# Output gates of a gated-linear-attention layer as one seven-product scheme on token tiles

## The chip, the cores and the metric

The kernel runs on one NeuronCore of a Trainium2 chip. The metric is the device time of one execution in microseconds (us). A core has a matrix engine (TensorE, "PE" in the profile; its weight loads are "PEld"), a vector engine (VectorE, "DVE"), a scalar engine (ScalarE, "ACT"), a general engine (GpSimd, "POOL") and an engine that here only issues transfers (SyncE, "SP"). Each has its own instruction queue, worked off in order. The engines share an on-chip memory; matmul results land in banks of 128 x 512 float32 numbers, from which DVE or ACT fetch them. Transfers (DMA) are issued from an engine's queue and run beside the engines.

## The reference

The computation is one layer of a decoder with 512 tokens and width 1024, in float32: a layer norm, then gated linear attention (GLA, 4 heads) and latent attention (MLA, 8 heads) side by side on the same normalised rows `h`, merged by two sigmoid gates, an output product, a layer norm, a squared-ReLU network of width 4096 and a last layer norm. What matters here is the GLA branch:

```python
q_g, k_g, v_g, r_g, a_lr, q_lat, kv_lat, gate_logits = jnp.split(h @ w_in, offsets, axis=-1)
log_a = log_sigmoid(a_lr @ w_gla_a2 + b_gla_a2) / 16
o_gla = gla_chunked(q_g * HK ** -0.5, k_g, v_g, log_a)      # per head
o_gla = rms_norm(o_gla, gla_norm_g)
y_gla = (o_gla * jax.nn.silu(r_g)) @ w_o_gla
```

`r_g`, the output gates, is the product of `h` (512 x 1024) and 1024 columns of `w_in` (1024 x 1024), and goes through silu. `v_g` has the same shape.

## The kernel before

**Products and pieces.** A float32 product is made of three matmuls on parts: each operand is split into a rounded high part and a low part, and high x high, high x low and low x high are summed in a bank. The parts of `h` are in `hT` (feature rows in partitions, tokens in columns). Weights come as a stream of pieces of 512 KB, planned in the order in which they are used (`plan`, `stream`). For each piece SP issues the load (`fetch`, two ahead of the piece in use), ACT writes the high part (`whi`, L189) and DVE the low part (`wlo`, L190). `pump(i)`, called where PE reaches piece i, emits the load and the split of the pieces that come next; the split of a piece is emitted one ahead, and `whi` and `wlo` have two buffers each.

**Stages.** In order: layer norm of the input; `lat` (the latent columns); `q`; `k`; then `v` and `r` in turn, half of the 1024 columns at a time: `proj_v(0)`, `proj_r(0)`, `proj_v(1)`, `proj_r(1)`; then the merge gates (`g`, and the units `g0` and `g1`), `y_gla`, MLA, the output product and the network.

**Token-tile products.** `proj_v` and `proj_r` use `gemm_tm` (L279 to L281): for each of 8 k-tiles of 128 features and each of 4 token tiles, three matmuls of 128x512, whose streaming operand is the weight. So one half of r is 4 pieces and 96 matmuls, 24 to a piece. The bank of a token tile is then read by `e`: ACT makes a tanh, and DVE two `scalar_tensor_tensor` that write the gates of two heads into `Rg[h]`.

**Work between the matmuls.** GLA's own work is written as generators: `gla_levels(h)` builds, per head, the decay masks in levels s = 2, 4, ..., 256 and the scores (POOL steps L680 and L681, ACT exponentials L686, DVE products M L688, small matmuls L742 and L746, masked copies L698 on DVE), and `gla_out(h)` multiplies scores with v and forms the gated rows. `spawn` puts a generator in a list, and `tick` lets the first few of them emit their next step; the products call `tick` every third token tile (`fine=3`). So the order of all engines' instructions is fixed when the program is built, by where the ticks fall; `finish` runs a generator to its end at that place.

**The seven-product scheme that is there already.** The units `g0`, `g1` compute a gate product from sums of operand blocks: the k rows and columns are taken as 2 x 2 blocks, and seven block products, with weights such as "12" plus "11" (t1), replace eight. The sums of weights are made by transfers: a load of one block, then an accumulating transfer from POOL's queue onto the same tile (`u_load`). The sums of `h` are made in `h_early`: per pair of k-tiles DVE adds and subtracts, splits each sum in two parts, and writes them to an off-chip scratch `hsd`, from which `h_load` reads them later. Results of products are combined in banks, and by ACT copies (L1072) and DVE additions or subtractions (L1068). Within g0 `tick(3)` is called after each second k.

Of the kernel before, what the change touches and what calls it, by code (L numbers as in the profile page):

```python
# [10 lines left out]
F32 = mybir.dt.float32  # L11
# [5 lines left out]
ALU = mybir.AluOpType  # L17
# [35 lines left out]
def tile_hybrid_block(ctx: ExitStack, tc: tile.TileContext, I, out, dbg=None):  # L53
# [23 lines left out]
    def B(shape, dt=F32, n="b"):  # L77
        return pb.tile(shape, dt, tag="B", name=nm(n))
# [4 lines left out]
    def DR(shape, n):  # L83
        n = nm(n)
        return pd.tile(shape, F32, tag=n, name=n)
# [7 lines left out]
    def f(ap):  # L93
        return ap.bitcast(F32)
# [207 lines left out]
        PL["lat", i] = plan("w_in", C_A + i * half, half, res=True)  # L302
    PL["q"] = plan("w_in", C_Q, T)
    PL["k"] = plan("w_in", C_K, T)
    for hp in range(2):
        PL["v", hp] = plan("w_in", C_V + hp * T, T)
        PL["r", hp] = plan("w_in", C_R + hp * T, T)
    def plan_qr(g):
        PL["qr", g] = plan("w_q_b", NOPE, 4 * ROPE, heads=(HQ, 4 * g, 4))

    PL["g", 0] = plan("w_in", C_G, T)

    WQ = {}
    HOME = {"w": ("whi", "wlo"), "r": ("wraw", "wraw"), "a": ("xh", "xl")}
    FMO = (("11", 0), ("21", 1), ("t1", 2), ("22", 5), ("t2", 3), ("t3", 6), ("t4", 4))
    HELD = (("21", "f1"), ("21", "g0"), ("22", "g0"))
# [329 lines left out]
                split(ps[:, i * HV:(i + 1) * HV], Vh[h][0][:, a, :], Vh[h][1][:, a, :])  # L646
        gemm_tm([PL["v", hp]], hT, T, e, guard=guard, fine=3)

    def proj_r(hp):
        hs = (2 * hp, 2 * hp + 1)  # L650

        def e(a, j, ps):
            th = B([P, T], F32, "th")
            act(th, ps, AF.Tanh, scale=0.5)
            for i, h in enumerate(hs):
                if Rg[h] is None:
                    Rg[h] = A([P, NT, HV], F32, "rg")
                stt(Rg[h][:, a, :], th[:, i * HV:(i + 1) * HV], 1.0, ps[:, i * HV:(i + 1) * HV],
                    op0=ALU.add, op1=ALU.mult)
        gemm_tm([PL["r", hp]], hT, T, e, fine=3)  # L660

    SS = [None] * GH

# [99 lines left out]
        yield  # L763

    def gla_out(h):
        while SS[h] is None or Vh[h] is None or Rg[h] is None:
            yield
        sd, s128, s256 = SS[h]

# [172 lines left out]
    hsd = []  # L942

    def h_early():
        for p in range(4):
            raw = [B([P, T], F32, "hraw") for _ in range(2)]
            for i in range(2):
                h = hT[2 * p + i]
                vtt(raw[i], f(h[:, 0]), f(h[:, 1]), op=ALU.add)
            yield  # L950
            a11, a12, a21, a22 = raw[0][:, :256], raw[1][:, :256], raw[0][:, 256:], raw[1][:, 256:]
            X = [B([P, 2, 256], F32, "hx") for _ in range(2)]
            vtt(X[0][:, 0], a21, a22, op=ALU.subtract)
            vtt(X[0][:, 1], X[0][:, 0], a11, op=ALU.subtract)
            vtt(X[1][:, 0], a12, X[0][:, 1], op=ALU.add)
            vtt(X[1][:, 1], a11, a21, op=ALU.subtract)
            yield
            for x in X:
                xs = [B([P, 2, 256], F32R, "sh") for _ in range(2)]
                split(x, *xs)  # L960
                hsd.append([DR([P, 2, 256], "hsd") for _ in range(2)])
                for t, d in zip(xs, hsd[-1]):
                    nc.sync.dma_start(d, f(t))
                yield

    t_ln1 = spawn(ln_in1())
# [1 line left out]
    for hf in range(2):  # L968
        if hf == 1:
            finish(t_ln1)  # L970
            t_prep = spawn(prep())
        for i in range(2):
            gemm_tm([PL["lat", i]], hT, half, ev_lat(i), tts=(2 * hf, 2 * hf + 1))
    t_lat = spawn(latents())
    gemm_fm(PL["q"], hT, T, ev_q)
    t_lat2 = spawn(latents2())
    t_he = spawn(h_early())
    gemm_fm(PL["k"], hT, T, ev_k)
    finish(t_prep, t_lat)
    lv = [False] * GH  # L980
# [15 lines left out]

    WID[0] = 3
    proj_v(0)
    proj_r(0)
    finish(t_lat2)  # L1000
    proj_v(1, lambda: levels_upto(1))
    proj_r(1)
    t_gla = [t_lv, t_out]


# [32 lines left out]
    def unit(key, ops, evac, after=None, pb=None):  # L1038
# [3 lines left out]
        def prod(op):  # L1042
            ph = dict(FMO)[op]
            opens = ph in (0, 2, 1)
            for g in range(UNITS[key][2]):
# [6 lines left out]
                for k in range(4):  # L1052
                    while len(ops) <= k:
                        tick(3)
                    xh, xl = ops[k][ph]
                    for a in range(2):
                        c = slice(a * P, (a + 1) * P)
                        oa = o[:, a * 256:(a + 1) * 256]
                        mm(oa, hi[:, k, c], xh, start=opens and k == 0 and a == 0, stop=False, skip_group_check=True)  # L1059
                        mm(oa, hi[:, k, c], xl, start=False, stop=False, skip_group_check=True)  # L1060
                        mm(oa, lo[:, k, c], xh, start=False, stop=k == 3, skip_group_check=True)  # L1061
                    if k % 2:
                        tick(3)
                if ph == 0:
                    e1[g] = B([P, T], F32, "e1")
# [45 lines left out]
    def h_load():  # L1111
        for p in range(4):
            o = {0: (0, 0), 1: (1, 0), 4: (1, 1)}
            o = {ph: tuple(part(hT[2 * p + i], w, slice(256 * h, 256 * h + 256)) for w in range(2))
                 for ph, (i, h) in o.items()}
            for i in range(2):
                xh, xl = [B([P, 2, 256], F32R, "sh") for _ in range(2)]
                for t, d in zip((xh, xl), hsd[2 * p + i]):
                    nc.sync.dma_start(f(t), d)
                o[(2, 5)[i]], o[(3, 6)[i]] = (xh[:, 0], xl[:, 0]), (xh[:, 1], xl[:, 1])  # L1120
            hops.append(o)
            yield

    finish(t_he)
    spawn(h_load())
    u_load("g0", "t1")
    u_load("g0", "22")
# [17 lines left out]
    prods = {"g0": unit("g0", hops, ev_gate0, after0), "g1": unit("g1", hops, ev_gate, after)}  # L1145
    for key, op in GATES:
        prods[key](op)
        if op == "t3" and key == "g0":
            finish(*t_gla)
    hT = hops = None  # L1150

# [380 lines left out]
```

## Time and profile before

| what | value |
|---|---|
| median of three runs | 893.7 us (893.48 to 894.96) |
| the profiled execution | 894.09 us, span 892.3 us |
| granted PE clock in it | 0.997 |
| PE busy | 875.2 us, 98% of the span |
| DVE busy | 619.0 us, 69% |
| ACT busy | 459.4 us, 51% |
| POOL busy | 168.0 us, 19% |
| bytes moved | 119.38 MB |

The span is the time from the first to the last instruction of the profiled execution; it lies within the time of the run. An instruction is named by its line, its engine, its operation, and by what it writes and reads (`wlo<-wraw,whi`); "px" and "mm" are result banks. A row of groups gives the busy time, the mean duration of one in ns, and the idle time of the engine before them with what ended it. Matmuls overlap in PE's pipeline, so the time that one costs is the distance between two starts, not its length. The line numbers are those of the kernel before; in the changed kernel those of the shared helpers are the same or 19 higher, and those behind the new functions some 95 higher.

### The profile page before, as it was taken

Reading aid. Unit: us, or ns where it says so; the run is one execution under the profiler, and the core shown is the slowest. Engines: PE = TensorE matmul, PEld = TensorE weight load, DVE = VectorE, ACT = ScalarE, POOL = GpSimd, SP = SyncE. Lnnn points to the kernel's source line nnn. Section 1 sums busy time; section 2 is a strip of 40 time slices with the busy share of each in tenths; the row PEclk is TensorE's granted clock in tenths of the full one; section 3 lists DMA queues with packets and bytes.
Section 4 is the critical chain, followed back from the end, with each engine's and each line's share of the span. In section 5 each row is a group of like instructions: output and inputs, shape, how many; then the busy total and the mean of one; then the engine's idle time right before and its main releaser. Section 6 shows DMA issues by size and latency. Waiting matters only on the chain.

```text
span 892.3 us, 12880 instructions
## 1 busy us (share of the span) xinstructions
PE 875.2 (98%) x4868; PEld 762.5 (85%) x4868; DVE 619.0 (69%) x1002; ACT 459.4 (51%) x808; POOL 168.0 (19%) x192
## 2 busy tenths in 40 slices
PE   6999999999999999999999999999999999999996
PEld 5988888888899988888888888988888888889985
DVE  7838987568365745657756797887556646787865
ACT  6456554455365543445644424365457546656720
POOL 1003555436120010100000002003500520131000
PEclk9999999999999999999999999999999999999998
DMA  7416632212997423121207618005950990399312
GB/s 247 121 47 200 225 119 72 71 48 68 305 272 195 124 89 112 38 60 54 96 24 273 197 48 306 2 1 122 308 136 9 273 257 29 79 230 235 118 65 79
DMA packets 80254, 119.38 MB, mean 134 GB/s; under 512 B 8464, under 2 KB 46224, under 8 KB 80192
## 3 DMA queue, kind: packets, MB, share of 16 engines
q1 hardware_dynamic: 63680, 85.54, 30.0%
q0 software_dynamic: 14592, 29.37, 14.7%
q10 hardware_dynamic: 1920, 3.66, 1.1%
q8 instruction: 38, 0.62, 0.3%
q14 instruction: 24, 0.20, 0.1%
HBM read 97.04 MB, written 8.91 MB: 119 GB/s over the span
## 4 chain that ended last, share of the span: by engine, by line
PE 94%; DVE 3%; DMA 1%; issue 1%; ACT 0%; POOLq 0%; DVEq 0%
PE mm L245 12%; PE mm L247 12%; PE mm L246 12%; PE mm L279 7%; PE mm L280 7%; PE mm L281 7%; PE mm L1061 3%; PE mm L1060 3%; PE mm L1059 3%; PE px L1344 2%; PE px L1345 2%; PE px L1343 2%; PE mm L1344 2%; PE mm L1345 2%; PE mm L1343 2%; PE px L742 2%
## 5 line engine op out<-in xcount | busy, mean ns | idle before, releaser
L190 DVE TENSOR_TENSOR wlo<-wraw,whi 128x1024 fp32r<-128x1024 f32 (+2 forms) x95 | 105.4, 1109 | 108.4 <-ACT whi L189 103.9
L189 ACT ACTIVATE whi<-wraw 128x1024 fp32r<-128x1024 f32 (+2 forms) x95 | 90.7, 955 | 89.5 <-PE mm L246 36.6
L245 PE MATMUL mm<-h,whi 128*128 128x512 f32 x256 | 99.9, 391 | 0.0
L246 PE MATMUL mm<-h,whi 128*128 128x512 f32 x256 | 99.9, 390 | 0.0
L247 PE MATMUL mm<-h,wlo 128*128 128x512 f32 x256 | 95.5, 389 | 0.0
L1362 POOL DMA_DIRECT2D res<-ev x42 | 37.3, 1008 | 179.0 <-ACT ev L1360 154.7
L190 DVE TENSOR_TENSOR wlo<-wq,whi 128x1024 fp32r<-128x1024 f32 x36 | 44.1, 1225 | 27.0 <-ACT whi L189 26.8
L247 PEld LDWEIGHTS mm<-h,wlo 128*128 128x128 f32 x256 | 48.1, 188 | 10.0
L245 PEld LDWEIGHTS mm<-h,whi 128*128 128x128 f32 x256 | 48.1, 188 | 9.7
L246 PEld LDWEIGHTS mm<-h,whi 128*128 128x128 f32 x256 | 48.1, 188 | 9.6
L189 ACT ACTIVATE whi<-wq 128x1024 fp32r<-128x1024 f32 x36 | 38.1, 1058 | 26.2 <-PE mm L1060 14.3
L279 PE MATMUL mm<-whi,h 128*128 128x512 f32 x128 | 50.7, 409 | 0.0
L280 PE MATMUL mm<-wlo,h 128*128 128x512 f32 x128 | 50.5, 395 | 0.0
L281 PE MATMUL mm<-whi,h 128*128 128x512 f32 x128 | 50.2, 394 | 0.0
L1060 PE MATMUL mm<-sh,whi 128*128 128x256 f32 x160 | 45.3, 283 | 0.0
L1059 PE MATMUL mm<-sh,whi 128*128 128x256 f32 x160 | 45.3, 283 | 0.0
L1061 PE MATMUL mm<-sh,wlo 128*128 128x256 f32 x160 | 45.3, 283 | 0.0
L189 ACT ACTIVATE xh<-wraw 128x1024 fp32r<-128x1024 f32 (+1 forms) x28 | 27.4, 987 | 29.2 <-PE mm L281 15.9
L190 DVE TENSOR_TENSOR xl<-wraw,xh 128x1024 fp32r<-128x1024 f32 (+1 forms) x28 | 31.3, 1130 | 9.6 <-ACT xh L189 9.5
L686 ACT ACTIVATE E<-rp 128x256 f32<-128x256 f32 x64 | 26.1, 417 | 22.7 <-POOL rp L681 13.9
L1405 ACT ACTIVATE relu<-mm 128x512 f32<-128x512 f32 x24 | 14.1, 596 | 41.8 <-PE mm L247 41.8
L409 POOL TENSOR_TENSOR mv<-mv,mhalf 128x1 f32<-128x1 f32 x4 | 3.3, 837 | 170.3 <-DVE mv L408 170.3
(433 smaller groups left out, 2662.8 us busy)
## 6 DMA issues: line engine op xcount, KB each, us to landing
wraw<-in_w_ff_dram SPq DMA_DIRECT2D x36, 512.0 KB, 5.2
wraw<-in_w_in_dram SPq DMA_DIRECT2D x35, 512.0 KB, 3.5
wq<-in_w_ff_dram POOLq DMA_DIRECT2D x26, 512.0 KB, 9.5
res<-ev POOLq DMA_DIRECT2D x42, 256.0 KB, 9.8
wq<-in_w_in_dram SPq DMA_DIRECT2D x10, 512.0 KB, 5.5
hsd<-sh SPq DMA_DIRECT2D x16, 256.0 KB, 2.6
sh<-hsd SPq DMA_DIRECT2D x16, 256.0 KB, 5.3
wraw<-in_w_o_gla_dram SPq DMA_DIRECT2D x8, 512.0 KB, 3.7
```

The source lines that it names most:

```text
L189: st["ins"] = act(hi[:, :nk, :n], raw[:, :nk, :n], AF.Copy)
L190: st["lo"] = vtt(lo[:, :nk, :n], raw[:, :nk, :n], f(hi[:, :nk, :n]), op=ALU.subtract)
L245: mm(o, hi[:, c], xh, start=first, stop=False)
L246: mm(o, hi[:, c], xl, start=False, stop=False)
L247: mm(o, lo[:, c], xh, start=False, stop=last)
L279: mm(o, xh, hi[:, :n], start=opens, stop=False, skip_group_check=share)
L280: mm(o, xh, lo[:, :n], start=False, stop=False, skip_group_check=share)
L281: mm(o, xl, hi[:, :n], start=False, stop=last, skip_group_check=share)
L1059: mm(oa, hi[:, k, c], xh, start=opens and k == 0 and a == 0, stop=False, skip_group_check=True)
L1060: mm(oa, hi[:, k, c], xl, start=False, stop=False, skip_group_check=True)
L1061: mm(oa, lo[:, k, c], xh, start=False, stop=k == 3, skip_group_check=True)
L1362: nc.gpsimd.dma_start(res[tt + t][:, j * T:(j + 1) * T], e, accum_op=ALU.add)
```

## The change

The two calls of `proj_r` become one. The 512 x 1024 x 1024 product of r is taken as 2 x 2 blocks in tokens (two halves of 256), k (even and odd k-tiles) and columns (two halves of 512), and done as seven block products in place of eight (`RW`: the weight operands 11, 21, t2, t1, t3, 22, t4, each with a phase that names its operand of `h`). A block product is two pieces, of 12 matmuls of 128x512 each (two k-tiles, two token tiles, three matmuls). So 14 pieces and 168 matmuls stand for 8 pieces and 192 matmuls.

- The weight sums t1 to t4 are made by transfers. `r_load` (SP) brings block 12 into the tiles of t2, t1 and t3, `r_acc` (POOL) accumulates blocks 11 and 22 on them: six loads and eight accumulating transfers, emitted by the generator `r_prep` in the second half of the latent product and after. t4 is t2 plus block 21: two more accumulating transfers onto t2's tiles, emitted after product t1 (`RA4`).
- `h_early` is emitted before q and not after it (it idles for six ticks first), splits per 256 columns (16 splits, 16 writes), and must be done before r. r reads the sums back into tiles "xr" (16 reads of 256 KB, one product ahead); `h_load` reads them again for g0 and g1, as before.
- Results are combined in two banks per token half, with six ACT copies ("er") and six DVE additions or subtractions on 128x512, and then go through the same tanh and products (`silu`).
- The order is v0, all of r, v1. `gla_out(h)` waits, at build time, until all four token tiles of its gates have been emitted (`rgn`). In r `tick` is called three times per product (`RT`).
- In g0 `tick(3)` is called only after the last k, and GLA's generators are finished after product t4 and not after t3.

The matmul count of the whole program falls by 24, all of 128x512; ACT gets 20 instructions more, DVE 20, SP 20 transfers, POOL 10.

```diff
@@ -302,15 +302,34 @@
         PL["lat", i] = plan("w_in", C_A + i * half, half, res=True)
     PL["q"] = plan("w_in", C_Q, T)
     PL["k"] = plan("w_in", C_K, T)
-    for hp in range(2):
-        PL["v", hp] = plan("w_in", C_V + hp * T, T)
-        PL["r", hp] = plan("w_in", C_R + hp * T, T)
+    WQ = {}
+
+    RY, RT, RA4 = (4, 4, 2, 2, 1, 2, 2), ((0, 0), (1, 0), (1, 1)), "t1"
+    RW = (("11", 0), ("21", 1), ("t2", 3), ("t1", 2), ("t3", 6), ("22", 5), ("t4", 4))
+
+    def r_src(op, hf):
+        i, j = int(op[0]) - 1, int(op[1]) - 1
+        c0 = C_R + j * T
+        return I["w_in"].rearrange("(k p) n -> p k n", p=P)[:, 4 * hf + i:4 * hf + i + 3:2, c0:c0 + T]
+
+    PL["v", 0] = plan("w_in", C_V, T)
+    PL["r"] = []
+    for op, _ in RW:
+        for hf in range(2):
+            PL["r"].append(len(stream))
+            e = {"nk": 2, "n": T, "res": False}
+            if op[0] == "t":
+                e["src"] = lambda q=("r", op, hf): WQ[q]
+            else:
+                e["dmas"] = [(slice(0, 2), r_src(op, hf), None)]
+            stream.append(e)
+    PL["v", 1] = plan("w_in", C_V + T, T)
+
     def plan_qr(g):
         PL["qr", g] = plan("w_q_b", NOPE, 4 * ROPE, heads=(HQ, 4 * g, 4))
 
     PL["g", 0] = plan("w_in", C_G, T)
 
-    WQ = {}
     HOME = {"w": ("whi", "wlo"), "r": ("wraw", "wraw"), "a": ("xh", "xl")}
     FMO = (("11", 0), ("21", 1), ("t1", 2), ("22", 5), ("t2", 3), ("t3", 6), ("t4", 4))
     HELD = (("21", "f1"), ("21", "g0"), ("22", "g0"))
@@ -646,18 +665,94 @@
                 split(ps[:, i * HV:(i + 1) * HV], Vh[h][0][:, a, :], Vh[h][1][:, a, :])
         gemm_tm([PL["v", hp]], hT, T, e, guard=guard, fine=3)
 
-    def proj_r(hp):
-        hs = (2 * hp, 2 * hp + 1)
-
-        def e(a, j, ps):
-            th = B([P, T], F32, "th")
-            act(th, ps, AF.Tanh, scale=0.5)
-            for i, h in enumerate(hs):
-                if Rg[h] is None:
-                    Rg[h] = A([P, NT, HV], F32, "rg")
-                stt(Rg[h][:, a, :], th[:, i * HV:(i + 1) * HV], 1.0, ps[:, i * HV:(i + 1) * HV],
-                    op0=ALU.add, op1=ALU.mult)
-        gemm_tm([PL["r", hp]], hT, T, e, fine=3)
+    def silu(j, a, ps):
+        th = B([P, T], F32, "th")
+        act(th, ps, AF.Tanh, scale=0.5)
+        for i in range(2):
+            h = 2 * j + i
+            if Rg[h] is None:
+                Rg[h] = A([P, NT, HV], F32, "rg")
+            stt(Rg[h][:, a, :], th[:, i * HV:(i + 1) * HV], 1.0, ps[:, i * HV:(i + 1) * HV],
+                op0=ALU.add, op1=ALU.mult)
+            rgn[h] += 1
+
+    rgn = [0] * GH
+
+    def r_acc(to, op):
+        for hf in range(2):
+            nc.gpsimd.dma_start(WQ["r", to, hf], r_src(op, hf), accum_op=ALU.add)
+
+    def r_load(to):
+        for hf in range(2):
+            t = WQ["r", to, hf] = A([P, 2, T], F32, "wq")
+            nc.sync.dma_start(t, r_src("12", hf))
+
+    def r_prep():
+        for (fn, *args), wait in zip(((r_load, "t2"), (r_acc, "t2", "11"), (r_load, "t1"), (r_acc, "t2", "22"), (r_load, "t3"),
+                                      (r_acc, "t1", "11"), (r_acc, "t3", "22")), RY):
+            fn(*args)
+            for _ in range(wait):
+                yield
+
+    def proj_r():
+        bank, e, xs = {}, {}, {}
+
+        def x_load(ph):
+            xs[ph] = []
+            for p in range(4):
+                t = B([P, 2, 256], F32R, "xr")
+                nc.sync.dma_start(f(t), hsd[p][(2, 3, 5, 6).index(ph)])
+                xs[ph].append((t[:, 0], t[:, 1]))
+
+        nat = {0: (0, 0), 1: (1, 0), 4: (1, 1)}
+        for n, (op, ph) in enumerate(RW):
+            if n + 1 < len(RW) and RW[n + 1][1] not in nat:
+                x_load(RW[n + 1][1])
+            if ph in nat:
+                i, h = nat[ph]
+                x = [tuple(hT[2 * p + i][:, w, 256 * h:256 * h + 256] for w in range(2)) for p in range(4)]
+            else:
+                x = xs.pop(ph)
+            opens = ph in (0, 1, 2)
+            for hf in range(2):
+                it = PL["r"][2 * n + hf]
+                pump(it)
+                hi, lo = stream[it]["w"]
+                for pp in range(2):
+                    xh, xl = x[2 * hf + pp]
+                    for t in range(2):
+                        key = ("a" if ph in (0, 3, 6, 4) else "b", t)
+                        if ph in (0, 1) and not hf and not pp:
+                            bank[key] = MM()
+                        o, c = bank[key], slice(t * P, (t + 1) * P)
+                        mm(o, xh[:, c], hi[:, pp], start=opens and not hf and not pp, stop=False, skip_group_check=True)
+                        mm(o, xh[:, c], lo[:, pp], start=False, stop=False, skip_group_check=True)
+                        mm(o, xl[:, c], hi[:, pp], start=False, stop=hf == 1 and pp == 1, skip_group_check=True)
+                    if (hf, pp) in RT:
+                        tick(None)
+            for t in range(2):
+                a, b = bank["a", t], bank.get(("b", t))
+                if ph in (0, 3, 2):
+                    e[ph, t] = B([P, T], F32, "er")
+                    act(e[ph, t], b if ph == 2 else a, AF.Copy)
+                elif ph == 1:
+                    vtt(e[0, t], b, e[0, t], op=ALU.add)
+                    silu(0, t, e[0, t])
+                elif ph == 6:
+                    vtt(e[2, t], e[2, t], a, op=ALU.subtract)
+                    silu(1, 2 + t, e[2, t])
+                elif ph == 5:
+                    vtt(e[3, t], b, e[3, t], op=ALU.subtract)
+                    silu(1, t, e[3, t])
+                else:
+                    silu(0, 2 + t, a)
+            if op == RA4:
+                r_acc4()
+
+    def r_acc4():
+        for hf in range(2):
+            WQ["r", "t4", hf] = WQ["r", "t2", hf]
+        r_acc("t4", "21")
 
     SS = [None] * GH
 
@@ -763,7 +858,7 @@
         yield
 
     def gla_out(h):
-        while SS[h] is None or Vh[h] is None or Rg[h] is None:
+        while SS[h] is None or Vh[h] is None or rgn[h] < NT:
             yield
         sd, s128, s256 = SS[h]
 
@@ -942,6 +1037,8 @@
     hsd = []
 
     def h_early():
+        for _ in range(6):
+            yield
         for p in range(4):
             raw = [B([P, T], F32, "hraw") for _ in range(2)]
             for i in range(2):
@@ -955,12 +1052,12 @@
             vtt(X[1][:, 0], a12, X[0][:, 1], op=ALU.add)
             vtt(X[1][:, 1], a11, a21, op=ALU.subtract)
             yield
-            for x in X:
-                xs = [B([P, 2, 256], F32R, "sh") for _ in range(2)]
-                split(x, *xs)
-                hsd.append([DR([P, 2, 256], "hsd") for _ in range(2)])
-                for t, d in zip(xs, hsd[-1]):
-                    nc.sync.dma_start(d, f(t))
+            hsd.append([DR([P, 2, 256], "hsd") for _ in range(4)])
+            for i, x in enumerate(X):
+                xs = [B([P, 2, 256], F32R, "hs") for _ in range(2)]
+                for e in range(2):
+                    split(x[:, e], xs[e][:, 0], xs[e][:, 1])
+                    nc.sync.dma_start(hsd[p][2 * i + e], f(xs[e]))
                 yield
 
     t_ln1 = spawn(ln_in1())
@@ -969,12 +1066,13 @@
         if hf == 1:
             finish(t_ln1)
             t_prep = spawn(prep())
+            t_rp = spawn(r_prep())
         for i in range(2):
             gemm_tm([PL["lat", i]], hT, half, ev_lat(i), tts=(2 * hf, 2 * hf + 1))
     t_lat = spawn(latents())
+    t_he = spawn(h_early())
     gemm_fm(PL["q"], hT, T, ev_q)
     t_lat2 = spawn(latents2())
-    t_he = spawn(h_early())
     gemm_fm(PL["k"], hT, T, ev_k)
     finish(t_prep, t_lat)
     lv = [False] * GH
@@ -996,10 +1094,10 @@
 
     WID[0] = 3
     proj_v(0)
-    proj_r(0)
+    finish(t_he, t_rp)
+    proj_r()
     finish(t_lat2)
     proj_v(1, lambda: levels_upto(1))
-    proj_r(1)
     t_gla = [t_lv, t_out]
 
 
@@ -1059,7 +1157,7 @@
                         mm(oa, hi[:, k, c], xh, start=opens and k == 0 and a == 0, stop=False, skip_group_check=True)
                         mm(oa, hi[:, k, c], xl, start=False, stop=False, skip_group_check=True)
                         mm(oa, lo[:, k, c], xh, start=False, stop=k == 3, skip_group_check=True)
-                    if k % 2:
+                    if k == 3 or k == 1 and key != "g0":
                         tick(3)
                 if ph == 0:
                     e1[g] = B([P, T], F32, "e1")
@@ -1113,15 +1211,13 @@
             o = {0: (0, 0), 1: (1, 0), 4: (1, 1)}
             o = {ph: tuple(part(hT[2 * p + i], w, slice(256 * h, 256 * h + 256)) for w in range(2))
                  for ph, (i, h) in o.items()}
-            for i in range(2):
-                xh, xl = [B([P, 2, 256], F32R, "sh") for _ in range(2)]
-                for t, d in zip((xh, xl), hsd[2 * p + i]):
-                    nc.sync.dma_start(f(t), d)
-                o[(2, 5)[i]], o[(3, 6)[i]] = (xh[:, 0], xl[:, 0]), (xh[:, 1], xl[:, 1])
+            for x, ph in enumerate((2, 3, 5, 6)):
+                t = B([P, 2, 256], F32R, "sh")
+                nc.sync.dma_start(f(t), hsd[p][x])
+                o[ph] = (t[:, 0], t[:, 1])
             hops.append(o)
             yield
 
-    finish(t_he)
     spawn(h_load())
     u_load("g0", "t1")
     u_load("g0", "22")
@@ -1145,7 +1241,7 @@
     prods = {"g0": unit("g0", hops, ev_gate0, after0), "g1": unit("g1", hops, ev_gate, after)}
     for key, op in GATES:
         prods[key](op)
-        if op == "t3" and key == "g0":
+        if op == "t4" and key == "g0":
             finish(*t_gla)
     hT = hops = None
```

## The prediction

> **What bounds the kernel now.** I read the page's busy shares, its 40 slices and its chain first, then PE's waits, and then the stretch that the change rewrites.
>
> ```profile
> span 892.3 us, 12880 instructions
> ...
> PE 875.2 (98%) x4868; PEld 762.5 (85%) x4868; DVE 619.0 (69%) x1002; ACT 459.4 (51%) x808; POOL 168.0 (19%) x192
> ...
> POOL 1003555436120010100000002003500520131000
> ...
> DMA  7416632212997423121207618005950990399312
> ...
> PE 94%; DVE 3%; DMA 1%; issue 1%; ACT 0%; POOLq 0%; DVEq 0%
> ```
>
> PE (TensorE's matmuls) is busy 98% of the span and carries 94% of the chain that ends last. So a matmul that goes is worth its full time, as long as the others never have to wait. The idle time of PE, by what it waited for:
>
> ```profile
> PE px L424 <- ACT x L413: 8.6, 1, 8.6
> PE px L742 <- DVE SD L734: 0.7, 1, 0.7
> PE mm L245 <- ACT h L427: 0.3, 1, 0.3
> PE px L746 <- DVE M L688: 0.2, 1, 0.2
> ```
>
> The first is the start-up; all that is left is 1.2 us. The kernel has hardly a wait that the change could win back; it can only remove PE work and add waits. By stretches (columns: us; then busy time and count of PE, PEld, DVE, ACT, POOL; granted clock; DMA share; GB/s):
>
> ```profile
> core 0: us, PE busy (x) PEld busy (x) DVE busy (x) ACT busy (x) POOL busy (x), PEclk, DMA share, GB/s
> 46.80:70.00 23.20, 23.20 (x105) 19.04 (x104) 8.17 (x11) 15.20 (x24) 3.83 (x3) 1.00 0.15 46
> ...
> 93.00:125.00 32.00, 31.02 (x174) 26.30 (x173) 31.78 (x60) 19.06 (x40) 17.49 (x21) 1.00 0.52 176
> 125.00:160.00 35.00, 35.00 (x191) 29.87 (x190) 25.85 (x44) 18.48 (x39) 19.50 (x21) 1.00 0.22 65
> 160.00:190.00 30.00, 30.00 (x182) 26.38 (x181) 18.06 (x33) 13.87 (x35) 13.64 (x15) 1.00 0.22 70
> 190.00:224.00 34.00, 34.00 (x197) 29.55 (x196) 25.00 (x47) 20.07 (x47) 18.58 (x21) 1.00 0.23 70
> 224.00:260.00 36.00, 36.00 (x216) 31.97 (x216) 14.34 (x23) 14.91 (x31) 7.43 (x7) 1.00 1.04 298
> ```
>
> The first row lies in the q product, the second is v0, and the next three hold r0, v1 and r1 with the GLA work between them. DVE (VectorE) is the second bound: 31.78 of 32 us in v0, then 25.85 + 18.06 + 25.00 = 68.9 of 99 us.
>
> **The change, part by part.** *Removed matmuls.* Per token half-product 12 matmuls of 128x512, 14 of them: 168 in place of 192, so 24 go. How far apart such matmuls start:
>
> ```profile
> 94.80 0.40 PE L280 MATMUL mm<-wlo,h 128*128 128x512 f32 x1
> ...
> 99.12 0.39 PE L281 MATMUL mm<-whi,h 128*128 128x512 f32 x1
> ```
>
> These two starts are 19 matmuls apart: 4.32 / 19 = 0.227 us each (the 0.39 us is a pipelined length). 24 x 0.227 = **-5.45 us**. The Trainium skill, "TensorE: Matmul & The Clock Gate", section "Back-to-back issue gap", has about 131 ns per matmul of N=512 in a sustained stream; by it the term would be 24 x 0.131 = 3.1 us. The trace does not agree (227 ns at a granted clock of 1.00), so the sum goes by the trace.
>
> *Added DVE work in the r stretch.* This decides. The rows, DVE's groups between 93 and 224 us, and one bank combine from the existing g1 scheme, which works as the new r does:
>
> ```profile
> L688 DVE TENSOR_TENSOR M<-E,qk 128x512 f32<-128x512 f32 x32 | 27.1, 846 | 6.6 <-ACT E L686 6.5
> L190 DVE TENSOR_TENSOR wlo<-wraw,whi 128x1024 fp32r<-128x1024 f32 x16 | 21.0, 1312 | 3.3 <-ACT whi L189 3.3
> ...
> L112 DVE TENSOR_TENSOR vl<-mm,vh 128x256 fp32r<-128x256 f32 x16 | 6.2, 415 | 3.0 <-ACT vh L111 2.9
> L658 DVE SCALAR_TENSOR_TENSOR rg<-th,mm 128x256 f32<-128x256 f32 x13 | 4.8, 415 | 1.2 <-ACT th L654 1.2
> ...
> L112 DVE TENSOR_TENSOR sh<-hx,sh 128x512 fp32r<-128x512 f32 x4 | 3.6, 892 | 0.0
> ```
> ```profile
> 286.39 0.69 DVE L1068 TENSOR_TENSOR e<-px,e 128x512 f32<-128x512 f32 x1 [0.68 <-PE px L1061]
> ```
>
> Each of the 14 weight pieces is split by ACT (hi) and DVE (lo); there were 8. So 6 x 1.31 = 7.9 us and 6 combines x 0.69 = 4.1 us are added: 68.9 + 12.0 = 80.9 us of DVE in 99 - 5.45 = 93.5 us. That fits on the whole, but r is now in one block. The built program's matmul order puts 13.0 us of GLA matmuls among r's 168 x 0.227 = 38.2 us, so r lasts 51.2 us (v1 then follows). In r DVE must do 14 x 1.31 = 18.4 (splits), 4.1 (combines) and 16 gate products x 0.415 = 6.6, together 29.1 us. Besides, it has the GLA work: 80.9 less 29.1, less v1's 4 splits (5.2) and 8 lo parts (3.3), is 43.3 us over 93.5, or 0.463 per us, 23.7 us in r. The sum is 52.8 us of DVE work in 51.2 us of PE work: **+1.6 us**, if DVE loses nothing else. (Counting the DVE instructions that the built program has between r's first split and v1's first, at the same means, gives 53.7, so +2.5; I keep the smaller, since the h operand work leaves v0 and DVE can begin r less behind.) From below: 0, were half the GLA masks (M) done before or after r. From above: bursts. After the products 21, t3 and 22 two combines and four gate products, 1.38 + 1.66 = 3.0 us, come at once: with its split (1.31) and GLA work (0.463 x 3.66 = 1.7) such a piece has 6.0 us of DVE work in 51.2 / 14 = 3.66 us, 2.4 too much; t4's has 4.7, 1.0 too much; the ten others have 3.0, 0.65 to spare. Two buffers per part let DVE work one piece ahead, so each burst can use about one such 0.65: 3 x 1.75 + 0.35 = 5.6 us.
>
> How tight a two-buffer piece is shows in g1, where 24 matmuls of 128x256 feed on one:
>
> ```profile
> 286.19 0.28 PE L1059 MATMUL mm<-sh,whi 128*128 128x256 f32 x1
> 286.31 1.06 ACT L189 ACTIVATE whi<-wq 128x1024 fp32r<-128x1024 f32 x1 [1.07 <-issue]
> 287.41 1.22 DVE L190 TENSOR_TENSOR wlo<-wq,whi 128x1024 fp32r<-128x1024 f32 x1 [0.33 <-ACT whi L189]
> ...
> 289.07 0.28 PE L1059 MATMUL mm<-sh,whi 128*128 128x256 f32 x1
> ```
>
> The split begins when PE opens a piece and ends 287.41 + 1.22 - 286.19 = 2.44 us later, before the next begins at 2.88. An r piece takes 12 x 0.227 = 2.73 us without GLA matmuls: 0.3 us of room for the bare chain, none for another DVE operation in it.
>
> *Hand-over from v0 to r.* In the kernel before:
>
> ```profile
> 124.64 0.39 PE L281 MATMUL mm<-whi,h 128*128 128x512 f32 x1
> ...
> 125.54 0.58 PE L279 MATMUL mm<-whi,h 128*128 128x512 f32 x1
> ```
> ```profile
> 126.09 1.46 DVE L671 COPY rp<-g 128x512 f32<-128x512 f32 x1
> ...
> 127.47 1.21 DVE L190 TENSOR_TENSOR wlo<-wraw,whi 128x1024 fp32r<-128x1024 f32 x1
> ```
>
> After v0's last matmul DVE finishes the second piece's lo at 128.68. The new r wants it at 125.54 + 2.73 + 0.227 = 128.50: **+0.2 us** (0 if a GLA matmul lies between, at most a split, 1.2).
>
> *ACT* gets 6 more hi conversions of 1.06 us and 6 bank copies, counted no dearer, 12.7 us at most, where it is busy 18.48 of 35 us: 0 on the path by itself; with that cover gone it is a link of the 2.44 us chain above.
>
> *Transfers.* Six loads and ten accumulating transfers of 512 KB make the sums; 16 readbacks of 256 KB feed r; two weight loads go.
>
> ```profile
> wq<-in_w_in_dram POOLq DMA_DIRECT2D x6, 512.0 KB, 8.2
> ...
> sh<-hsd SPq DMA_DIRECT2D x16, 256.0 KB, 5.3
> ```
> ```profile
> L1362 POOL DMA_DIRECT2D res<-ev x42 | 37.3, 1008 | 179.0 <-ACT ev L1360 154.7
> ```
>
> Eight accumulates and the six loads go out in the latent and q products (about 25 to 60 us), where POOL's digits are 0 and DMA's 4 and 1: 8 x 1.0 us of issue and 7 MB in idle queues, some 65 us ahead of use: 0. t4's two accumulates stand in POOL behind DVE's splits of t2, at about 146 us, and are wanted at about 165. With 8.2 us to land some 10 us are left. On POOL they push the GLA level steps queued behind them back by 2 x 1.0 us; POOL is busy 19.50 of 35 us there, so between 0 and 2.0 us reach M and PE; I take 0, as PE waited for M once in the whole run, 0.2 us. The readbacks are issued on SP one product (over 5 us) ahead, about their 5.3 us; DMA share is 0.22: 0, from above 1 us at the first.
>
> *The h operand sums*, moved ahead of q, take 16 lo splits of 256 columns (0.415 each, 6.6 us) instead of 8 of 512 (0.892, 7.1 us). DVE has 23.2 - 8.17 = 15 us free in the first row of the stretches: 0; from above one late q piece, a split. v0's DVE load falls by at least the quoted 3.6 us. r now waits for these sums and the transfers to have been emitted, which is an order and not a wait on the chip.
>
> *g0 and GLA's end.* Fewer ticks in g0 and a later finish move GLA matmuls, none is added: 0. Stretch 224 to 260 has the DMA full (share 1.04, 298 GB/s) while PE stays at 36.00 of 36; PE will come 3.6 us earlier.
>
> **Sum.** -5.45 + 1.6 + 0.2 = -3.65 us. The profiled execution took 894.09 us (its span and 1.8 us around it), 0.4 above the median of 893.7: 890.4 on its own time, **890.1 us** on the median.
>
> **Rivals.** *The bursts are lost one by one, and the time is the same.* Stall 5.6 + 0.2 gives +0.35, 894.0 us. For it: DVE's 31.78 of 32 us in v0 show that it can be the pacer; the room of 0.3 us. Against it: in v0 so full a DVE cost PE but 0.98 us. A like result, 893.7, would come if the full DMA of 224 to 260 kept its pace and held PE up by what r won; against it stands PE's full row there.
>
> *DVE's splits stretch beside POOL, and it is slower.* DVE operations are longer while POOL works on the same memory:
>
> ```profile
> 93.81 0.42 DVE L671 COPY rp<-g 128x512 f32<-128x512 f32 x1
> ...
> 94.38 1.70 POOL L680 TENSOR_TENSOR rp<-rp 128x256 f32<-128x256 f32 x1 [8.44 <-DVE rp L671]
> ...
> 101.46 1.88 DVE L190 TENSOR_TENSOR wlo<-wraw,whi 128x1024 fp32r<-128x1024 f32 x1
> ```
> ```profile
> 125.52 1.29 POOL L760 TENSOR_TENSOR sd<-SD,sd 128x512 fp32r<-128x512 f32 x1 [4.29 <-ACT sd L759]
> ```
>
> The same copy took 0.42 us while POOL had been idle for 8.44 us, and 1.46 us (quoted above) when that POOL operation ran; a split took 1.88 instead of 1.2. A DVE that never rests in r meets POOL's level steps oftener. All 14 splits at 1.88 add 14 x 0.57 = 8.0 us: -5.45 + 1.8 + 8.0 = +4.35, **898.0 us**. It decides from a stall of 7.25 us on, which is a mean split of 1.31 + (7.25 - 1.8) / 14 = 1.70 us. Against it: the mean of 1312 ns was taken with POOL already busy over half the time. The Trainium skill, "SBUF — State Buffer", section "SBUF: two separate sides", says that DVE and GpSimd share a port pair as an exclusive lock, for which a DVE operation with two SBUF inputs competes with a GpSimd one that reads SBUF. The trace agrees as far as 0.42 against 1.46 us and 1.2 against 1.88 us go; by that rule the stretch grows with overlap, the rival's mechanism.
>
> *t4's sums come late.* They would have to land 10 us later than 8.2; a landing of 20 us would cost 2 us: 892.1.
>
> *Nothing stalls* (DVE's GLA work shifts out of r): -5.45, 888.2 us.
>
> **How the numbers follow.** 0.2% of 893.7 is 1.8 us, about what a measurement of this kernel can tell from no change. Forecast with the no-stall end, 888.2 to 891.9: 0.61. Burst or DMA rival (stall 3.65 to 7.25; 891.9 to 895.5): 0.15. Late t4: 0.02, the time hardly changed. Stretched DVE or any stall over 7.25: 0.22. So faster 0.61, same 0.17, slower 0.22. The range 888.0 to 897.0 takes in the no-stall end and most of the slower case, leaving out some 0.1 above and little below; the forecast's own is 888.2 to 891.9.
>
> **What would show it.** Right: 168 matmuls in r at 0.227 us; PE waits between 125 and 177 us of about 2 us together, on DVE's lo splits and at product ends; DVE busy over 95% there, splits near 1.3 us; y_gla starting some 3.6 us earlier and all behind it shifted alike. Wrong: waits on ACT's hi parts or on readbacks; splits over 1.7 us; PE waits over 4 us in r, or new ones before 125 us (q late through the h sums) or in 224 to 300 us.

## The result, and the profile after

The changed kernel takes 891.44 us (median of 8 runs, 890.81 to 891.96) against 893.75 us before (8 runs): a ratio of 0.9973, 95% interval 0.9962 to 0.9984. It is faster by 2.3 us; forecast were 3.6. The profiled execution has a span of 890.0 us, 2.3 less than before. So of the 5.45 us of removed matmuls 3.1 are missing. Where? Three of PE's starts cut the run into parts: its first matmul, the first of v0, and the first of `y_gla`, behind everything that the change touches. The timeline of PE, first before, then after:

```profile
8.57 0.48 PE L424 MATMUL px<-ca,x 128*128 128x128 f32 x1 [8.57 <-ACT x L413]
...
93.80 0.48 PE L279 MATMUL mm<-whi,h 128*128 128x512 f32 x1
...
319.31 0.40 PE L245 MATMUL mm<-ogT,whi 128*128 128x512 f32 x1
```
```profile
9.37 0.48 PE L443 MATMUL px<-ca,x 128*128 128x128 f32 x1 [9.37 <-ACT x L432]
...
94.60 0.48 PE L279 MATMUL mm<-whi,h 128*128 128x512 f32 x1
...
317.13 0.40 PE L245 MATMUL mm<-ogT,whi 128*128 128x512 f32 x1
```

From the first matmul to v0 both take the same (85.23 us). From v0 to `y_gla` it was 225.51 us and is 222.53: 2.98 won, so 5.45 - 2.98 = 2.47 us are lost in that stretch. The other 0.80 us are lost before the first matmul, which starts at 9.37 instead of 8.57. (Behind the last instruction of the engines another 0.16 us are won, which makes the 3.1.) The program of this start is the same; what differs is DVE's wait for an input tile (timeline of DVE, before and after):

```profile
6.49 0.69 DVE L406 BATCH_NORM_STATS2 bst<-x 128x6 f32<-128x512 f32 x1 [0.54 <-DMA x<-in_x_dram]
```
```profile
7.28 0.69 DVE L425 BATCH_NORM_STATS2 bst<-x 128x6 f32<-128x512 f32 x1 [1.38 <-DMA x<-in_x_dram]
```

The lost 2.47 us lie in r and in what directly follows it: v0 takes 31.83 us, 31.74 before, and from r's first matmul to the first of `g` (126.43 to 217.90 us) the same matmuls take 91.47 us here and 88.77 in the run without lo splits below. The windows of 125 to 177 us, before and after (columns as in the prediction):

```profile
125.00:177.00 52.00, 52.00 (x280) 44.61 (x279) 34.25 (x59) 25.20 (x58) 27.09 (x30) 1.00 0.23 71
```
```profile
125.00:177.00 52.00, 51.26 (x278) 43.36 (x277) 49.87 (x72) 35.22 (x72) 37.31 (x36) 1.00 0.53 158
```

DVE goes from 34.25 to 49.87 of 52 us, POOL from 27.09 to 37.31. PE's waits between 126 and 185 us, by what it waited for, are all for DVE:

```profile
PE mm L729 <- DVE wlo L190: 0.5, 2, 0.3
PE px L837 <- DVE M L783: 0.3, 1, 0.3
PE px L845 <- DVE SD L793: 0.2, 1, 0.2
```

They sum to 1.0 us; the waits that the view does not list as such stretch the starts of matmuls by tenths. DVE's groups of 125 to 182 us, before and then after, show how its operations grew:

```profile
L688 DVE TENSOR_TENSOR M<-E,qk 128x512 f32<-128x512 f32 x14 | 12.4, 888 | 3.3 <-ACT E L686 3.3
L190 DVE TENSOR_TENSOR wlo<-wraw,whi 128x1024 fp32r<-128x1024 f32 x8 | 10.0, 1251 | 2.0 <-ACT whi L189 1.9
...
L658 DVE SCALAR_TENSOR_TENSOR rg<-th,mm 128x256 f32<-128x256 f32 x8 | 2.9, 413 | 1.2 <-ACT th L654 1.2
```
```profile
L783 DVE TENSOR_TENSOR M<-E,qk 128x512 f32<-128x512 f32 x16 | 15.8, 990 | 0.6 <-ACT E L781 0.6
L190 DVE TENSOR_TENSOR wlo<-wq,whi 128x1024 fp32r<-128x1024 f32 x8 | 11.2, 1400 | 0.8 <-ACT whi L189 0.8
L675 DVE SCALAR_TENSOR_TENSOR rg<-th,er 128x256 f32<-128x256 f32 x12 | 7.1, 634 | 0.0
L190 DVE TENSOR_TENSOR wlo<-wraw,whi 128x1024 fp32r<-128x1024 f32 x5 | 6.8, 1363 | 0.4 <-ACT whi L189 0.4
```

Nothing idles long any more, and every operation with two operands in memory is longer: masks M 990 ns (888), splits 1363 to 1400 (1251), gate products that read the copy "er" 634, where those that read a bank took 413.

### The profile page after: what moved, and what is told of

The parts are those of the page before. It is cut to its first block, busy times and chain, and to the rows that moved or that the text cites. A ratio compares the mean times of both kernels' runs of the same rounds, so it can differ in the third digit from the quotient of the medians.

```text
span 890.0 us, 12974 instructions
## 1 busy us (share of the span) xinstructions
PE 871.3 (98%) x4844; PEld 757.1 (85%) x4844; DVE 634.6 (71%) x1022; ACT 467.0 (52%) x828; POOL 186.8 (21%) x202
## 4 chain that ended last, share of the span: by engine, by line
PE 89%; DVE 6%; issue 2%; ACT 1%; POOL 1%; DMA 1%; POOLq 0%; DVEq 0%; SPq 0%
PE mm L245 12%; PE mm L247 12%; PE mm L246 12%; PE mm L281 5%; PE mm L280 5%; PE mm L279 5%; PE mm L1159 3%; PE mm L1158 3%; PE mm L1157 3%; PE px L1441 2%; PE px L1439 2%; PE px L1440 2%; PE mm L1441 2%; PE mm L1439 2%; PE mm L1440 2%
## 5 line engine op out<-in xcount | busy, mean ns | idle before, releaser
L190 DVE TENSOR_TENSOR wlo<-wraw,whi 128x1024 fp32r<-128x1024 f32 (+2 forms) x93 | 102.5, 1102 | 102.9 <-ACT whi L189 98.5
L189 ACT ACTIVATE whi<-wraw 128x1024 fp32r<-128x1024 f32 (+2 forms) x93 | 88.5, 952 | 93.1 <-PE mm L246 44.8
L190 DVE TENSOR_TENSOR wlo<-wq,whi 128x1024 fp32r<-128x1024 f32 x44 | 55.3, 1256 | 25.2 <-ACT whi L189 25.2
L189 ACT ACTIVATE whi<-wq 128x1024 fp32r<-128x1024 f32 x44 | 46.5, 1056 | 24.9 <-PE mm L1158 11.9
L775 POOL TENSOR_TENSOR rp<-rp 128x256 f32<-128x256 f32 x32 | 31.5, 983 | 25.8 <-ACT E L781 14.4
L776 POOL TENSOR_TENSOR rp<-rp 128x256 f32<-128x256 f32 x32 | 31.7, 989 | 8.7 <-ACT q L806 5.9
L783 DVE TENSOR_TENSOR M<-E,qk 128x512 f32<-128x512 f32 x32 | 29.5, 925 | 3.3 <-ACT E L781 3.3
```

Source lines behind the costliest of these rows:

```text
L189: st["ins"] = act(hi[:, :nk, :n], raw[:, :nk, :n], AF.Copy)
L190: st["lo"] = vtt(lo[:, :nk, :n], raw[:, :nk, :n], f(hi[:, :nk, :n]), op=ALU.subtract)
```

## The experiments

**Theory D:** DVE's work paces r and costs PE about 2.4 us there. Within it, **theory P:** what makes it too much is that POOL's level steps stretch DVE's operations. Rivals: **C**, ACT's conversions or the banks pace r; **S**, the change itself delays the start; **bursts** at product ends. The measure beside the time is the stretch from v0 to `y_gla`, which the start does not enter: 225.51 us before, 222.53 after, 220.06 if nothing were lost.

**The same kernel again.**

> The changed kernel once more, unchanged, as the base for the others. Theory D (DVE's work in r costs PE about 2.4 us there, and the other 0.8 us is a second input tile that happened to land late in the profiled run): 891.4 us within 0.6, PE's first wait anywhere between 8.5 and 9.5 us. Rival S (the change itself delays the start): the first wait is 9.4 us again.

891.5 us, ratio 0.9976 [0.9966, 0.9985]. The first matmul starts at 8.85 us this time and the stretch is again 222.53 us (94.28 to 316.81). So the same program starts 0.5 us apart in two executions: S, a start that is always late, falls, and the 2.47 us are the same in both.

**No lo splits in r.**

```diff
-            e = {"nk": 2, "n": T, "res": False}
+            e = {"nk": 2, "n": T, "res": False, "nolo": True}
...
-                st["lo"] = vtt(lo[:, :nk, :n], raw[:, :nk, :n], ...)
+                if lo is not None:
+                    st["lo"] = vtt(lo[:, :nk, :n], raw[:, :nk, :n], ...)
...
-                        mm(o, xh[:, c], lo[:, pp], ...)
+                        mm(o, xh[:, c], hi[:, pp], ...)
```

> The changed kernel without DVE's 14 lo splits of r's weights (the middle one of the three matmuls takes the high part again, so PE does the same number of matmuls and the low part's share of r is left out). Takes some 18 us of DVE work out of r. Theory D: PE's stalls in r go, 889.0 to 889.6 us, waits of PE between 125 and 185 us under 0.3 us. Rival C (ACT's hi conversion, the bank copies or the banks pace r, not DVE): within 0.5 us of the unchanged kernel. Rival S: 891 us as well.

889.09 us, ratio 0.9948 [0.9934, 0.9961]. PE's starts:

```profile
93.89 0.48 PE L281 MATMUL mm<-whi,h 128*128 128x512 f32 x1
...
313.93 0.40 PE L247 MATMUL mm<-ogT,whi 128*128 128x512 f32 x1
```

220.04 us: 5.47 less than before, 24 x 0.228. With DVE out of the way the whole price of the removed matmuls comes, though ACT still makes all 14 hi parts and all copies. C falls, D stands. That the two agree to 0.02 us is partly chance: v0 took 32.04 us in this execution, 0.30 more than before, so from r's first matmul on it is 5.77.

**No POOL level steps.**

```diff
         def advance(s):
-            Rv, Pv = pairs(rp[:, 0, :], s), pairs(rp[:, 1, :], s)
...
-            gtt(Pv[:, :, 1, :], Pv[:, :, 1, :], ..., op=ALU.add)
+            pass
```

> The changed kernel without POOL's 64 level steps (left out: the running sums of GLA's gate logarithms; all else stays, and DVE does the same operations). Theory P (DVE's two-operand work is stretched beside POOL's): lo splits in r near 1.21 us (1.3 to 1.4 now), masks M near 0.69 (0.93 now), gate products near 0.42, DVE busy in r 4 to 6 us less, and 889.2 to 890.2 us. Without P: the durations stay, 891.5 less at most 0.5.

887.6 us, ratio 0.993 [0.9916, 0.9943]. DVE's groups of 125 to 182 us:

```profile
L780 DVE TENSOR_TENSOR M<-E,qk 128x512 f32<-128x512 f32 x16 | 10.6, 689 | 0.4 <-ACT E L778 0.4
L190 DVE TENSOR_TENSOR wlo<-wq,whi 128x1024 fp32r<-128x1024 f32 x8 | 9.8, 1221 | 3.1 <-ACT whi L189 3.1
L190 DVE TENSOR_TENSOR wlo<-wraw,whi 128x1024 fp32r<-128x1024 f32 x7 | 8.6, 1233 | 3.3 <-ACT whi L189 3.3
...
L675 DVE SCALAR_TENSOR_TENSOR rg<-th,er 128x256 f32<-128x256 f32 x12 | 4.5, 417 | 0.0
```

DVE does the same operations, and each is back at its short time: M 689, splits 1221 to 1233, gate products 417. Against the changed kernel that is 16 x 0.30 + 13 x 0.16 + 12 x 0.22 = 9.5 us of DVE durations in r which POOL's work had cost. PE has no wait left between 20 and 330 us, and the stretch is 218.64 us (94.79 to 313.43): the 5.45 us, and 1.4 us that the kernel before loses as well, mostly in v0 (31.74 us there, 30.38 here; the prediction read 0.98 us off PE's busy time). The edit also takes away the delay of the level chain itself; so the durations, and not the time, are what speaks for P.

**E in a bank.** POOL works on; only where DVE's mask product reads one operand from changes.

```diff
-            E = B([P, T], F32, "E")
+            E = PX(n="E") if rgn[0] < NT else B([P, T], F32, "E")
```

> The changed kernel with ACT writing GLA's exponentials E into a result bank (of those that r leaves free) until r is done, so that DVE's mask product M reads one operand from memory and one from a bank. POOL does all its level steps. Theory P (what POOL stretches are DVE operations that read two operands from memory): M in r falls from 0.99 to about 0.69 us, 16 x 0.3 = 4.8 us of DVE less, 889.3 to 890.3 us. Without P (any DVE operation beside POOL is stretched): M stays over 0.9 and the time at 891.5. A rival that would hide it: too few banks, level steps wait, 892 or more.

890.78 us, ratio 0.9964 [0.9951, 0.9976]; the stretch is 221.87 us (95.37 to 317.24). The masks, and what PE then waits for:

```profile
L783 DVE TENSOR_TENSOR M<-E,qk 128x512 f32<-128x512 f32 x15 | 10.2, 681 | 0.2
```
```profile
PE mm L279 <- DVE rg L675: 1.2, 1, 1.2
PE px L837 <- DVE M L783: 0.4, 1, 0.4
```

M is 681 ns beside a working POOL: with one operand in a bank it is not stretched. That settles P's mechanism. The time moves less, as a new wait stands in v1: not its first matmul (178.37 us) but one at 189.58 us waits 1.2 us for the gate products of r's last product, which still read its bank. (In the run below that copies this product out, the wait is gone.)

**Combines written into the bank**, so that eight gate products read one operand from a bank.

```diff
-                    vtt(e[0, t], b, e[0, t], op=ALU.add)
-                    silu(0, t, e[0, t])
+                    vtt(b, b, e[0, t], op=ALU.add)
+                    silu(0, t, b)
...
-                    vtt(e[3, t], b, e[3, t], op=ALU.subtract)
-                    silu(1, t, e[3, t])
+                    vtt(b, b, e[3, t], op=ALU.subtract)
+                    silu(1, t, b)
```

> The combines after the products 21 and 22 write into the result bank and not into the copy, so that eight of the gate products in r read one operand from memory and one from a bank, as they did before the change. Theory P (gate products with both operands in memory are stretched by POOL's work: 634 ns here, 415 ns before): these eight fall to about 0.42 us, some 2 us of DVE work less, and 890.5 to 891.3 us. Theory D without P (only the count of DVE operations matters): the durations stay near 0.63 us and the time at 891.5.

890.83 us, ratio 0.9965 [0.9952, 0.9977]; stretch 221.54 us. One view shows both kinds side by side, under the same POOL:

```profile
L675 DVE SCALAR_TENSOR_TENSOR rg<-th,mm 128x256 f32<-128x256 f32 x8 | 3.0, 406 | 0.0
L675 DVE SCALAR_TENSOR_TENSOR rg<-th,er 128x256 f32<-128x256 f32 x4 | 2.6, 700 | 0.0
```

**No combines in r.**

```diff
-                    vtt(e[0, t], b, e[0, t], op=ALU.add)
...
-                    vtt(e[2, t], e[2, t], a, op=ALU.subtract)
...
-                    vtt(e[3, t], b, e[3, t], op=ALU.subtract)
```

> The changed kernel without the six additions and subtractions that combine the banks in r (left out: the combination; copies, tanh and gate products stay). Takes 6 x 0.69 = 4.1 us of DVE work out, at the ends of products. Theory D: about half of the 2.4 us come back, 890.0 to 890.6 us. The rival of my prediction, bursts at product ends: nearly all of it, 889.2 to 889.6. Rival C: 891.4.

893.17 us, ratio 0.9989 [0.998, 0.9999]: every theory missed. DVE has less to do and the stretch is longer, 224.02 us. The planner, which fixes each engine's order when the program is built, puts the freed gate products in one block ahead of a split (DVE's timeline and PE's waits):

```profile
165.93 3.24 DVE L675 SCALAR_TENSOR_TENSOR rg<-th,er 128x256 f32<-128x256 f32 x4
...
169.62 1.25 DVE L190 TENSOR_TENSOR wlo<-wraw,whi 128x1024 fp32r<-128x1024 f32 x1
```
```profile
PE mm L729 <- DVE wlo L190: 2.7, 3, 1.0
```

That is the burst of my rival, made by the order and not by the sum of the work: DVE is in order, and a split behind 3.24 us of work that nobody needs yet comes late. In the changed kernel the same four products (2.58 us, from 168.48 us) stand behind that split, which starts at 164.76.

**The h sums really early.**

```diff
-        for _ in range(6):
+        for _ in range(2):
...
-    t_he = spawn(h_early())
+    t_he = h_early()
+    active.insert(0, t_he)
```

> The h operand sums put first in the list of generators from q on, so that they really end before v0 (in the changed kernel the last of them is at 119 us, as before the change). Theory D with what my prediction took for granted (v0's relief lets DVE begin r less behind): 0.5 to 1 us faster than 891.5, DVE busy in v0 under 28 of 32 us. Rival: DVE's backlog at the start of r is not what r's stalls hang on, 891.5 within 0.4, or slower where POOL's accumulating transfers and the earlier sums meet in q (waits of PE before 94 us).

895.02 us, ratio 1.0011 [1.0002, 1.002]. The stretch from v0 on gets shorter, 222.23 us, and DVE's busy time in v0 falls from 31.32 of 31.80 us to 25.59 of 31.40 (the sums' last split ends at 102.5 us, still in v0); but from the first matmul to v0 it is 3.8 us longer (89.00 us), most of it in one wait:

```profile
PE mm L245 <- ACT qk L543: 2.7, 1, 2.7
```

k's matmuls wait for ACT to fetch q's banks, which now stands behind other work on ACT; the granted clock is 0.50 from 73.0 to 76.3 us, at the end of this wait and behind it. The 0.3 us that are won from v0 on lie in v0 itself (31.40 us, not 31.83); from r's first matmul to `g` it is 91.60 us, not 91.47. So DVE's relief in v0 is worth nothing in r, as the rival said.

**The order alone.** The kernel before with v0, r0, r1, v1; the weight pieces are planned in that order too.

```diff
     proj_r(0)
+    proj_r(1)
     finish(t_lat2)
     proj_v(1, lambda: levels_upto(1))
-    proj_r(1)
```

> The kernel before with the new order alone (v0, r0, r1, v1; r in eight block products as before). Theory D: the order costs nothing by itself, 893.7 us within 0.8. A rival (part of the lost gain is due to v1 coming later than GLA's levels want it): 894.8 us or more.

897.5 us, ratio 1.0044 [1.0031, 1.0056]; the stretch is 228.77 us, 3.26 more than before. The largest wait is of GLA's output products for ACT:

```profile
PE px L786 <- ACT osq L790: 1.8, 1, 1.8
```

They and a head's last level matmuls come in one go between r1's last matmul (189.17 us) and v1's first (196.52), with no matmuls of a projection to cover them. Behind the wait the granted clock is 0.50 from 193.5 to 196.9 us, which by an estimate (half of 3.4 us) costs another 1.7: together 3.5, about the 3.26. In the changed kernel neither is listed, and in the run without lo splits, in the same new order, the full price of the matmuls came, so there the order by itself costs PE nothing that shows.

**r behind v1.**

```diff
-    proj_r()
     finish(t_lat2)
     proj_v(1, lambda: levels_upto(1))
+    proj_r()
```

The weight pieces are planned in the same new order.

> The order v0, v1, r: the seven-product r moves behind v1, into a stretch where DVE had 30% to spare. The order v0, r, v1 alone cost 3.4 us in the eight-product kernel, mostly where GLA's output waits. Theory O (part of that cost is still in the changed kernel): 889.5 to 890.8 us, waits of PE on DVE in r under 0.5 us. Rival: GLA's outputs then come so late that their tail stands in g0 and g1, with DVE and ACT waits there: 892 us or more.

909.63 us, ratio 1.0169 [1.0152, 1.0186]. The rival's case: GLA's outputs end at 290 us instead of 266, and g0 stands behind them. These are the largest waits; the granted clock behind them is 0.51 (255 to 262 us) and 0.50 (292.6 to 296 us):

```profile
PE px L1157 <- ACT whi L189: 5.9, 1, 5.9
PE px L900 <- DVE og L894: 3.3, 1, 3.3
```

**Three attempts at more**: both bank edits together; the in-bank combines with two ticks per product, `RT = ((0, 0), (1, 0))`; and E in a bank with the last product copied out by ACT before its gate products:

```diff
-                    silu(0, 2 + t, a)
+                    e4 = B([P, T], F32, "er")
+                    act(e4, a, AF.Copy)
+                    silu(0, 2 + t, e4)
```

> Both: E in a bank and the combines after products 21 and 22 in the bank. Theory P: 888.6 to 889.8 us, PE waits in r under 0.6 us, close to the full 5.45 us below the kernel before. Without P: 890.8 or more.

> The in-bank combines and two ticks per product in r instead of three, which moves a third of GLA's steps, and the POOL and DVE work with them, from r to v1. If r's stalls only need less DVE work per us: 889.8 to 890.6 us. Rival: the levels are then run down at the end of v1 in one go, as v1's guard asks, and PE waits there: 892 us or more.

> The kernel with E in a bank (masks near 0.68 us), and in addition the last product's result copied out by ACT, so that v1's first matmul, which waited 1.2 us for a gate product to release its bank, finds it free. If the wait was only that bank: 889.4 to 890.3 us. Rival: with DVE still nearly full, the planner's other order of the queues puts the same microsecond elsewhere, 890.6 us or more.

893.03 us (0.9985 [0.9976, 0.9994]), 893.65 (0.9994 [0.9985, 1.0003]) and 893.23 (0.9995 [0.9986, 1.0004]): all missed. Each has one wait of about 2 us in a new place: of the level matmuls for M at r's end, of g0 for ACT's hi part, and of the level matmuls for M just behind v1's end.

```profile
PE px L837 <- DVE M L783: 2.4, 2, 2.0
```
```profile
PE px L1157 <- ACT whi L189: 2.2, 1, 2.2
```
```profile
PE px L839 <- DVE M L785: 2.3, 2, 2.0
```

The place of the first, DVE and then PE, and the window around it:

```profile
178.15 1.22 DVE L190 TENSOR_TENSOR wlo<-wraw,whi 128x1024 fp32r<-128x1024 f32 x1
...
179.28 0.44 DVE L793 COPY_PREDICATED SD<-lmask,px 96x256 f32<-96x256 uint8 x1
179.61 0.68 DVE L783 TENSOR_TENSOR M<-E,qk 128x512 f32<-128x512 f32 x1
...
180.44 0.65 PE L837 MATMUL px<-M 128*64 128x64 f32 x8 [1.99 <-DVE M L783]
```
```profile
177.00:190.00 13.00, 11.00 (x61) 9.36 (x61) 6.76 (x16) 6.35 (x14) 5.30 (x8) 0.87 0.28 81
```

DVE's 6.76 of 13 us are misleading: during the wait, from 178.4 to 180.4 us, it is busy 2.00 of 2.00. M stands behind a split of 1.22 us for v1, and between r's last matmul and v1's first (176.54 and 181.10 us) only the level matmuls themselves are left to PE. In the third, too, a split (1.26 us) stands ahead of the M that PE waits for. So it is again the order in DVE's queue; which step of the planner makes it stays open.

The wait is paid nearly twice. Behind it the granted clock falls, 0.87 in that row and 0.50 from 181.3 to 184.7 us, where matmuls start 0.43 us apart and not 0.228: about 1.7 us more, by an estimate from these numbers. The third has the same (0.51 from 213.5 to 217.0 us), the second not. Without wait and clock the first would be at 893.03 - 2.0 - 1.7 = 889.3 us, by the same estimate, where P forecast 888.6 to 889.8; no run shows it.

So no version was found that is clearly better; the two single bank edits are 0.6 us below the changed kernel, within their intervals.

## Why the prediction was right or wrong

The direction, the place and the mechanism held; the stall was too small.

- *Removed matmuls, -5.45:* right. With DVE relieved 5.47 came, 0.228 us each. The 131 ns of the Trainium skill ("TensorE: Matmul & The Clock Gate", "Back-to-back issue gap") would have made 3.1; no run here agrees with it.
- *DVE in r, +1.6:* the term that was mis-sized; the loss, with the hand-over, is 2.47. I took durations from stretches where DVE rested. M was priced at 846 ns and took 990, the gate products at 415 and twelve of them took 634, because they now read a copy in memory and not a bank; splits at 1312 took 1363 to 1400. That the sum still came within 0.7 us of the loss is in part luck. By durations, DVE's operations from r's first matmul to v1's first (126.43 to 180.75 us) add up to 59.2 us and not 52.8; 29.5 of them are work other than r's own, for which I had 23.7. Against 51.2 us of PE work that would be a stall of 8.0. But durations can't be added up: the records overlap (a split of 131.87 + 1.23 = 133.10 us is followed by an operation that starts at 133.01), and DVE was busy 52.49 of 54.32 us. Durations that were too short and an overlap that was left out nearly cancelled.
- *Hand-over, +0.2:* no wait of PE at that place is listed; 0.
- *The h sums leave v0:* wrong. Their last split ended at 119.7 us before and ends at 121.1 after; the generator is spawned earlier, but the ticks there step only the first two in the list. DVE's 31.78 of 32 us in v0 became 31.79. The run that does it wins 0.4 us in v0, nothing in r, and has a dearer wait in k.
- *Transfers, 0:* right. t4's accumulating transfers were issued at 141.3 and 146.6 us, landed at 146.9 and 153.3, and the first split of t4 began at 172.1: 19 us to spare, not 10. The 224 to 260 stretch stayed at 36.00 of 36 us of PE.
- *Rivals:* the slower one had the right mechanism at a smaller size: the splits' mean rose to 1.39 us, where 1.70 would have decided it. For it, the Trainium skill's "SBUF — State Buffer", section "Who interferes with whom", is finer than what I quoted: a DVE operation with two inputs in memory competes with a POOL operation that reads it, one with at most one such input, outside DVE's 2-port modes, does not. The trace agrees, 700 against 406 ns in one kernel. Of the two signs that I gave for the rule only the split is a case of its first half; the copy (0.42 against 1.46 us) has a single input and was stretched all the same. The burst rival is real too, as the run without combines shows, but in the changed kernel the order holds it small.
- *The start, not in my sum:* the profiled execution lost 0.80 us there, which is scatter: 8.57, 9.37, 8.85, 8.52 and 9.34 us in five executions. In all twelve profiles with the new r it starts between 8.44 and 9.37 us, in the two with the old at 8.57 and 8.90.

## What to carry to other kernels

When a change saves work on the full engine by adding work on another, price the other engine's operations at the durations that they have when both it and the engine that stretches it (here POOL) are busy, not at the mean of a calmer stretch, and count the engine's busy time, not the sum of durations, where its records overlap. Where an operand moves from a bank to memory, count the operation anew. In a stretch where an in-order engine is near full, its order decides as much as its load: less work in a worse order was slower.

## What the runs showed that I had not expected

- DVE operations with one operand in a bank keep their time beside POOL (M 681 ns, gate products 406), those with two in memory do not (M 990, gate products 634 to 700): 9.5 us over r.
- Leaving six operations out of DVE's queue made the kernel 1.7 us slower, and moving v1 behind r1 alone cost 3.3 us: both through the order of the queues.
- In the profiled executions with a PE wait of 1.8 us or more, the granted clock fell to 0.50 for 3.4 us or longer in five of six (waits of 1.8, 2.0, 2.0, 2.7, and of 5.9 and 3.3 in one); behind a wait of 2.2 us in the sixth it did not, and behind the waits of 1.2 us or less in r and v1 it did not either. What decides it was not tried. A wait of 2 us can so cost nearly 4.
- PE's first matmul starts anywhere from 8.4 to 9.4 us, with the landing of one input tile: in a single profiled execution that can hide a third of an effect of this size, so stretches between two of PE's starts compare better than spans.
